# Feed-forward of a two-layer trunk: PSUM banks dealt out anew, five of seven weight operands and the activation sums copied through three of them

## The chip, the cores and the metric

The kernel runs on one core of a Trainium2 chip. TensorE (PE) multiplies, VectorE (DVE), ScalarE (ACT) and GpSimd (POOL) do the work on elements, and DMA queues, most of them issued by SyncE (SP), bring the weights from HBM. The metric is the device time of one execution in microseconds (us), as the median of repeated runs; lower is better. A profile is one such execution, recorded instruction by instruction.

## The reference, cut to what matters

The program is two layers of an attention mixer followed by a gated feed-forward with a causal convolution of width 3. 512 tokens, model width 1024, inner width 2816, all in fp32. The change touches the feed-forward only:

```python
def conv_ffn(h, w_gu, conv_w, conv_b, w_down):
    a, u = jnp.split(h @ w_gu, 2, axis=-1)
    a = causal_depthwise_conv(a, conv_w, conv_b)
    return (jax.nn.silu(a) * u) @ w_down

def reference(x, ...):
    for i in range(DEPTH):
        ...
        h = rms_norm(x, norm_ffn[i])
        x = x + conv_ffn(h, ffn_w_gu[i], ffn_conv_w[i], ffn_conv_b[i], ffn_w_down[i])
    return rms_norm(x, norm_final)
```

## The kernel before, in words

**Precision.** Every fp32 operand of a product is split into a high part, cast by ACT to the fp32r type, and a low part, the operand minus its high part, made by a subtraction on DVE or POOL. A product is three kinds of matmul: high with high, high with low, low with high. Tiles named h.. or wh are high parts, l.. or wl low parts.

**Feed-forward.** The inner width is cut into 22 column tiles f = 0 to 21 of 128. Of each, the gate half a and the up half u are wanted, 128 x 512 each. Tiles f = 0 to 2 take the plain way (gate_up, L205 for the matmuls): 24 matmuls of 512 columns for a and 24 for u. Tiles f = 3 to 21 (19 in a layer, 38 in all) take gate_up_7: tokens are cut into halves and the 2 x 2 product of (weight halves) x (token halves) is made with seven products instead of eight, numbered o = 0 to 6, each 12 matmuls of 256 columns (L619), 84 in all. Their left operands are the weights a1, a2, u1, u2 themselves (each 256 KB by its own DMA, L591) and sums of them: POOL makes s1 = u1 + u2, s2 = s1 - a1, s3 = a1 - u1, s4 = a2 - s2 (L596), of which s2 and s3 lie side by side in the tile "wraw". Each of the seven operands that is used (a1, s2, s3, a2, s1, s4, u2) is cast by ACT (L602) and subtracted by DVE (L608). The right operands are sums of the activations, built once in a layer while the plain tiles run (operands, L564 on): DVE scales, POOL makes four sums in a step, ACT casts (L579) and copies each pair of sums into a PSUM bank (L583), DVE subtracts (L585, tile "xs").

**After the products** of a tile f, in the order o = 0, 1, 3, 5, 2, 6, 4 into the four accumulators pa, pb, pc, pa, pb, pd, pc: ACT copies pa twice into the padded row tile "apad" (L629, L637), DVE adds the others (L623), ACT and DVE form the convolution in a PSUM tile py (L536, L537, L538), ACT applies Silu (L539), and POOL multiplies with u (L649, after which the result lies in g, xh or xl). After f = 21 the down projection follows, again with L205 matmuls into "mm" tiles; its operands are split on ACT (L670) and DVE (L671).

**PSUM.** All eight banks are in four rings: "mm" of 2, "s" of 2, "t" of 3 and "o" of 1. Every allocation with a tag takes the ring's next bank and waits until its former holder has been read for the last time. Which instruction stands where on an engine is decided by a scheduler when the program is built; SP issues the DMAs in an order that this also sets, and a DMA into a buffer waits in SP's queue for the last reader of that buffer's former content.

**What the change touches.** In `weights` (L588 on) the subtraction of a1 reads a copy of a1 that ACT has put in an "mm" bank, that of a2 a copy in "s", that of u2 a copy in "t" (L607). Those of s2, s3, s1 and s4 read both operands from SBUF. The accumulators pa, pb, pc, pd are in "mm", "s", "t", "o"; py is in "t", prs (the broadcast norm that L569 reads) in "t", and the copies of the activation sums go through the one bank of "o".

Of the kernel before, what the change touches and what calls it, by code (L numbers as in the profile page):

```python
# [11 lines left out]
F32 = mybir.dt.float32  # L12
# [5 lines left out]
P = 128  # L18
T = 512
# [12 lines left out]
B_MM, B_S, B_T, B_O = 2, 2, 3, 1  # L32
# [27 lines left out]
PLO = ((3, 6, 7), (3, 6))  # L60
BUFS = dict(a1=2, a2=2, u1=2, u2=2, s1=2, s4=2, ha1=2, la1=2, ha2=1, la2=1, hs1=1, ls1=1, hs4=1, ls4=1, hu2=1, lu2=1)
GL = [n for n in ("u1", "a1", "u2", "a2", "s1", "s4", "ha1", "la1", "ha2", "la2", "hs1", "ls1", "hs4", "ls4") for _ in range(BUFS[n])]
BANKS = dict(a1=("mm", B_MM), a2=("s", B_S), u2=("t", B_T))
CUES = (((), (0, 1), (2, 3, -1), (4, 5), (6, 7), (), ()), ((), (0, 1, 2), (3,), (4, 5, 6, -1), (7, 8), (), ()))
SCALE_SWA = "vvvv"
WARM_NSA, WARM_SWA = (54, 66)
# [73 lines left out]
def trunk(ctx: ExitStack, tc: tile.TileContext, x, w_nsa, w_gate, w_c1, w_c2, w_nsao, w_nsao3, w_swa, w_swao,  # L140
# [350 lines left out]
    with tc.tile_pool(name="tab", bufs=1) as pool:  # L491
        stats0 = ffn(tc, 0, locals())
        with tc.tile_pool(name="swa", bufs=1) as pool:
            cs = pool.tile([P, 2, T], F32, name="cs")
            vb = pool.tile([P, P], F32, name="vb")
            with tc.high_priority(offset=100):
                nc.sync.dma_start(cs, tabs)
                nc.sync.dma_start(vb, swa_vb)
            layer_now[0] = 1
            stats = Stats(pool, nc.gpsimd)  # L500
            swa(tc, locals())
            first = first_products(1, stats)
    ffn(tc, 1, locals())


def ffn(tc, layer, e):
    nc, wp, ps, V = e["nc"], e["wp"], e["ps"], e["V"]
# [4 lines left out]
    with tc.tile_pool(name=f"ffn{layer}", bufs=1) as pool:  # L512
# [3 lines left out]
        def conv(i):  # L516
            return conv_t[:, i:i + 1]
# [4 lines left out]
        def gated(f):  # L522
            k = f - NF + len(x_tags)
            n = f"g{f}" if k < 0 else f"{x_tags[k][0]}{x_tags[k][1]}"
            g[f] = (pool if k < 0 else e["cp"]).tile([P, T], F32, name=n, tag=n)
            return g[f]
# [5 lines left out]

        def activate(f, a):
            y = pool.tile([P, T], F32, name="y", tag="y", bufs=1)
            py = ps.tile([P, T], F32, name="t", tag="t", bufs=B_T)
            nc.scalar.activation(py, a[:, 2:], AF.Identity, scale=conv(f * 3 + 2), bias=conv(3 * NF + f))  # L536
            nc.vector.scalar_tensor_tensor(py, a[:, 1:T + 1], conv(f * 3 + 1), py, op0=ALU.mult, op1=ALU.add)  # L537
            nc.vector.scalar_tensor_tensor(py, a[:, 0:T], conv(f * 3), py, op0=ALU.mult, op1=ALU.add)  # L538
            nc.scalar.activation(y, py, AF.Silu)  # L539
            return y  # L540
# [6 lines left out]
        def gate_up(f):  # L547
            pa = plain(f, 0, "mm") if f else e["first"][0]
            a = apad[f % 2]
            nc.vector.tensor_tensor(a[:, 2:], pa, rstd, op=ALU.mult)  # L550
            y = activate(f, a)
            pu = plain(f, 1, "s") if f else e["first"][1]
            u = gated(f)
            nc.vector.tensor_tensor(u, pu, rstd, op=ALU.mult)
            nc.gpsimd.tensor_tensor(u, u, y, op=ALU.mult)
# [5 lines left out]
        def half(n, dt=F32R):  # L561
            return pool.tile([P, T], dt, name=n, tag=n, bufs=BUFS[n])

        def operands(i):  # L564
            n = [half(t, F32) for t in (("ha2", "hs4"), ("la2", "ls4"))[i % 2]]
            t = [half(t, F32).rearrange("p (o t) -> p o t", o=2) for t in (("hs1", "hu2"), ("ls1", "lu2"))[i % 2]]
            for h in range(2):
                k = i + h * NK // 2
                nc.vector.scalar_tensor_tensor(n[h], X[k], V(f"ffn{layer}", k), prs, op0=ALU.mult, op1=ALU.mult)  # L569
            x1l, x1r, x2l, x2r = (n[h][:, c] for h in range(2) for c in HALVES)  # L570
            t2, t1, t3, t4 = (t[j][:, h] for j in range(2) for h in range(2))
            eng = nc.gpsimd
            eng.tensor_tensor(t1, x1r, x1l, op=ALU.subtract)
            eng.tensor_tensor(t3, x2r, x1r, op=ALU.subtract)
            eng.tensor_tensor(t2, x2r, t1, op=ALU.subtract)
            eng.tensor_tensor(t4, x2l, t2, op=ALU.subtract)
            for o, src in ((slice(0, 1), x1l.unsqueeze(1)), (slice(5, 7), n[1].rearrange("p (o t) -> p o t", o=2)),
                           (slice(1, 3), t[0]), (slice(3, 5), t[1])):
                nc.scalar.copy(xs[:, o, i, 0], src)  # L579
                if o.stop - o.start == 2:  # L580

                    src2 = ps.tile([P, T], F32, name="o", tag="o", bufs=B_O).rearrange("p (o t) -> p o t", o=2)
                    nc.scalar.copy(src2, src)  # L583
                    src = src2
                nc.vector.tensor_tensor(xs[:, o, i, 1], src, f32(xs[:, o, i, 0]), op=ALU.subtract)  # L585

        def weights(f):
            a1, a2, u1, u2, s1, s4 = (half(n, F32) for n in ("a1", "a2", "u1", "u2", "s1", "s4"))  # L588
            for j, h, w in ((0, 0, a1), (1, 0, u1), (1, 1, u2), (0, 1, a2)):
                with tc.high_priority(offset=100):  # L590
                    nc.sync.dma_start(w, e["w_gu"][layer, j, f, :, h * T:(h + 1) * T])  # L591
            s23, l23, h23 = (wp.tile([P, 2, T], t, name=n, tag=n) for n, t in (("wraw", F32), ("wl", F32R), ("wh", F32R)))
            s2, s3 = (s23[:, h] for h in range(2))
            for out, x, y, op in ((s1, u1, u2, ALU.add), (s2, s1, a1, ALU.subtract), (s3, a1, u1, ALU.subtract),
                                  (s4, a2, s2, ALU.subtract)):
                nc.gpsimd.tensor_tensor(out, x, y, op=op)  # L596
            ws = {1: (h23[:, 0], l23[:, 0]), 3: (h23[:, 1], l23[:, 1])}
            for o, n, w in ((0, "a1", a1), (1, None, s2), (3, None, s3), (5, "a2", a2), (2, "s1", s1), (6, "s4", s4),
                            (4, "u2", u2)):
                if n:  # L600
                    ws[o] = half("h" + n), half("l" + n)
                nc.scalar.copy(ws[o][0], w)  # L602
                if n in BANKS:

                    tag, bufs = BANKS[n]
                    w = ps.tile([P, T], F32, name=tag, tag=tag, bufs=bufs)
                    nc.scalar.copy(w, {"a1": a1, "a2": a2, "u2": u2}[n])  # L607
                nc.vector.tensor_tensor(ws[o][1], w, f32(ws[o][0]), op=ALU.subtract)  # L608
            return ws

        def gate_up_7(f, cue):
            ws = weights(f)
            pa, pb, pc, pd = (ps.tile([P, T], F32, name=n, tag=n, bufs=b)[:, :H]
                              for n, b in (("mm", B_MM), ("s", B_S), ("t", B_T), ("o", B_O)))

            def product(pt, o, start=False):
                ops = [(0, x, i) for i in range(NK // 2) for x in range(2)] + [(1, 0, i) for i in range(NK // 2)]
                for n, (w, x, i) in enumerate(ops):
                    nc.tensor.matmul(pt, ws[o][w][:, i * P:(i + 1) * P], xs[:, o, i, x], start=start and n == 0,  # L619
                                     stop=n == len(ops) - 1, skip_group_check=True)  # L620

            def add(dst, pt, src):
                nc.vector.tensor_tensor(dst, pt, src, op=ALU.add)  # L623

            a, u = apad[f % 2], gated(f)
            al, ar = a[:, 2:2 + H], a[:, 2 + H:]
            ul, ur = (u[:, c] for c in HALVES)
            product(pa, 0, True)
            nc.scalar.copy(ar, pa)  # L629
            cue(0)  # L630
            product(pb, 1, True)
            add(ul, pb, ar)
            cue(1)
            product(pc, 3, True)
            cue(2)
            product(pa, 5)
            nc.scalar.copy(al, pa)  # L637
            cue(3)
            product(pb, 2)
            add(ar, pb, ar)  # L640
            add(ur, pc, ar)
            cue(4)
            product(pd, 6, True)
            add(ar, pd, ar)
            cue(5)
            product(pc, 4)
            add(ul, pc, ul)
            cue(6)
            nc.gpsimd.tensor_tensor(u, u, activate(f, a), op=ALU.mult)  # L649

        prs = ps.tile([P, T], F32, name="t", tag="t", bufs=B_T)
        nc.scalar.copy(prs, rstd)
        for f in range(PLAIN[layer]):
            gate_up(f)
# [25 lines left out]
        def cue(n):  # L680
            for f in CUES[layer][n]:
                if f < 0:
                    w_down.append(load_down(0, -1 - f))
                else:
                    split_g(f)
# [879 lines left out]
```

## Time and profile before

| | |
|---|---|
| median of three runs | 1295.8 us (1295.52 to 1297.48) |
| the profiled execution | 1297.73 us, span 1295.9 us |
| mean granted clock of TensorE | 0.982 |
| PE busy | 1228.0 us, 95% |
| DVE busy | 939.0 us, 72% |
| ACT busy | 760.1 us, 59% |
| POOL busy | 604.7 us, 47% |
| feed-forward of layer 0, tiles f = 3 on | about 405 to 626 us |
| feed-forward of layer 1, tiles f = 3 on | about 947 to 1167 us |

PE's share is a mean over stages. What the change can move is read in the two feed-forward stretches: how many matmuls PE gets done there in a stretch of time, what it waits for, and how the engines that make its operands follow one another.

### The profile page before, as it was taken

What the parts mean: (1) busy time and instruction counts of PE and PEld (TensorE: products, weight loads), DVE (VectorE), ACT (ScalarE), POOL (GpSimd) and SP (SyncE); (2) the same over time, 40 slices, a digit from 0 to 9 for tenths busy, and PEclk for the clock granted to TensorE, in tenths of its full rate; (3) what the DMA queues carried; (4) which work ended last, traced back from release to release, by engine and by line L of the source; (5) the groups of instructions that cost most, each with busy time, mean ns of one, the idle gap of its engine ahead of it and who ended that gap; (6) DMA issues with size and microseconds to landing.
All of it is one profiled execution on the core that took longest, in us unless ns stands there. A gap on an engine that the chain in (4) does not pass through costs nothing.

```text
span 1295.9 us, 20370 instructions
## 1 busy us (share of the span) xinstructions
PE 1228.0 (95%) x7246; PEld 1058.7 (82%) x7246; DVE 939.0 (72%) x1799; ACT 760.1 (59%) x1584; POOL 604.7 (47%) x451
## 2 busy tenths in 40 slices
PE   7999999989998999999999998999989999999997
PEld 5867986877876999999888886778779999998886
DVE  6376777978688897999633367897888999994223
ACT  4276667767558666767422225866677676683222
POOL 4494554523239676664100137322577766730002
PEclk9999999989998999999999998999989999999999
DMA  5856635041232332332233345322423332223333
GB/s 196 227 159 191 199 103 153 26 142 37 62 104 99 95 103 92 104 92 62 80 99 90 108 156 157 106 82 90 132 75 97 98 106 92 81 69 90 95 101 122
DMA packets 66485, 141.70 MB, mean 109 GB/s; under 512 B 8528, under 2 KB 16976, under 8 KB 66384
## 3 DMA queue, kind: packets, MB, share of 16 engines
q1 hardware_dynamic: 65008, 139.25, 35.5%
q8 instruction: 57, 0.93, 0.3%
q10 hardware_dynamic: 1376, 1.15, 0.3%
q14 instruction: 44, 0.36, 0.1%
HBM read 123.14 MB, written 17.24 MB: 108 GB/s over the span
## 4 chain that ended last, share of the span: by engine, by line
PE 53%; DVE 19%; DMA 7%; POOL 7%; ACT 7%; issue 5%; SPq 1%; POOLq 0%; DVEq 0%; ACTq 0%
PE mm L205 29%; PE t L619 4%; PE s L619 3%; DVE wl L608 3%; PE mm L619 3%; DMA u<-in_w_gu 2%; PE s L1165 2%; POOL s L596 2%; DVE ls L608 2%; PE o L619 2%; PE o L1007 2%; PE t L1189 2%; POOL wraw L596 1%; DMA d<-rh 1%; PE o L1307 1%
## 5 line engine op out<-in xcount | busy, mean ns | idle before, releaser
L182 ACT CAST wh<-wraw 128x1024 fp32r<-128x1024 f32 (+3 forms) x132 | 122.2, 926 | 224.5 <-PE mm L205 139.2
L183 DVE TENSOR_TENSOR wl<-wraw,wh 128x1024 fp32r<-128x1024 f32 (+3 forms) x80 | 98.0, 1225 | 118.7 <-PE mm L205 72.2
L183 POOL TENSOR_TENSOR wl<-wraw,wh 128x1024 fp32r<-128x1024 f32 (+3 forms) x52 | 98.7, 1902 | 136.5 <-PE mm L205 67.2
L205 PE MATMUL mm<-xs,wh 128*128 128x512 f32 (+1 forms) x374 | 141.5, 382 | 0.0
L238 POOL TENSOR_TENSOR rt<-rt 128x512 f32<-128x512 f32 x22 | 31.5, 1430 | 192.2 <-ACT rt L232 192.0
L608 DVE TENSOR_TENSOR wl<-wraw,wh 128x512 fp32r<-128x512 f32 x76 | 97.2, 1282 | 18.8 <-ACT wh L602 18.6
L205 PE MATMUL mm<-xh,wh 128*128 128x512 f32 x248 | 102.1, 413 | 6.9 <-ACT wh L182 5.1
L205 PE MATMUL mm<-xl,wh 128*128 128x512 f32 x248 | 99.9, 404 | 2.1 <-DVE xl L306 2.0
L619 PE MATMUL mm<-xs,ha 128*128 128x256 f32 x608 | 92.5, 289 | 9.4 <-ACT apad L629 4.8
L619 PEld LDWEIGHTS mm<-xs,ha 128*128 128x128 f32 x608 | 81.8, 195 | 12.3 <-ACT apad L629 6.2
L205 PE MATMUL mm<-xs,wl 128*128 128x512 f32 (+1 forms) x374 | 90.6, 382 | 0.0
L602 ACT CAST wh<-wraw 128x512 fp32r<-128x512 f32 x76 | 46.8, 620 | 69.4 <-POOL wraw L596 57.2
L1175 ACT ACTIVATE p<-p,sm 128x128 f32<-128x128 f32 (+3 forms) x128 | 71.7, 562 | 20.1 <-DVE sm L1172 19.5
L205 PEld LDWEIGHTS mm<-xs,wh 128*128 128x128 f32 x374 | 70.3, 188 | 14.7
L608 DVE TENSOR_TENSOR ls<-s,hs 128x512 fp32r<-128x512 f32 x76 | 80.2, 1060 | 0.0
L205 PEld LDWEIGHTS mm<-xs,wl 128*128 128x128 f32 x374 | 67.7, 188 | 15.1
L1172 DVE CUSTOM_DVE_ANT_0 p<-s,cst 128x128 f32<-128x128 f32 (+3 forms) x128 | 58.3, 480 | 18.1 <-PE t L1189 10.4
L205 PE MATMUL mm<-xh,wl 128*128 128x512 f32 x248 | 67.7, 403 | 0.0
L596 POOL TENSOR_TENSOR s<-u,u 128x512 f32<-128x512 f32 x38 | 53.2, 1401 | 27.1 <-DMA u<-in_w_gu 21.5
L649 POOL TENSOR_TENSOR xl<-xl,y 128x512 f32<-128x512 f32 x16 | 29.6, 1852 | 77.4 <-ACT y L539 69.9
L205 PEld LDWEIGHTS mm<-xh,wh 128*128 128x128 f32 x248 | 48.5, 196 | 18.8 <-ACT wh L182 5.3
L596 POOL TENSOR_TENSOR s<-a,wraw 128x512 f32<-128x512 f32 x38 | 62.8, 1653 | 0.2
(369 smaller groups left out, 3689.1 us busy)
## 6 DMA issues: line engine op xcount, KB each, us to landing
u<-in_w_gu SPq DMA_DIRECT2D x76, 256.0 KB, 2.9
a<-in_w_gu SPq DMA_DIRECT2D x76, 256.0 KB, 2.8
wraw<-in_w_dn SPq DMA_DIRECT2D x34, 512.0 KB, 3.5
wraw<-in_w_nsa SPq DMA_DIRECT2D x19, 512.0 KB, 4.9
q<-d SPq DMA_DIRECT2D x32, 256.0 KB, 5.1
wraw<-in_w_dn SPq DMA_DIRECT2D x17, 384.0 KB, 3.1
wraw<-in_w_gu SPq DMA_DIRECT2D x12, 512.0 KB, 3.5
d<-rh SPq DMA_DIRECT2D x21, 256.0 KB, 2.2
```

Source lines behind the costliest of these rows:

```text
L182: nc.scalar.copy(wh[:, c], raw[:, c])
L183: (eng or lo_eng[0]).tensor_tensor(wl[:, c], raw[:, c], f32(wh[:, c]), op=ALU.subtract)
L205: nc.tensor.matmul(pt, ws[k][w], rs[k][r], start=first and i == 0, stop=last and i == len(ops) - 1, **kw)
L238: self.eng.tensor_tensor(self.acc, self.acc, sq, op=ALU.add)
L596: nc.gpsimd.tensor_tensor(out, x, y, op=op)
L602: nc.scalar.copy(ws[o][0], w)
L608: nc.vector.tensor_tensor(ws[o][1], w, f32(ws[o][0]), op=ALU.subtract)
L619: nc.tensor.matmul(pt, ws[o][w][:, i * P:(i + 1) * P], xs[:, o, i, x], start=start and n == 0, stop=n == len(ops) - 1, skip_group_check=True)
L649: nc.gpsimd.tensor_tensor(u, u, activate(f, a), op=ALU.mult)
L1007: nc.tensor.matmul(acc[0][:, j * P:], v2[:, 2 * j + br], pp[:, 4 * j:4 * j + NT - j, :], start=br == 0 and j == 0 and pp is pts[0][0], sto ...
L1172: nc.vector.tensor_tensor_reduce(pt[:, c], pss[:, c], mask[:, T - (c.stop - c.start):], -1.0, 3e38, ALU.add, ALU.min, st[:, u:u + 1])
L1175: nc.scalar.activation(pt[:, c], pt[:, c], AF.Exp, scale=-1.0, bias=st[:, u:u + 1], accum_out=st[:, 2 + u:3 + u])
```

## The change

All that the change does is to move tiles between the four rings and to add copies. Of the seven weight operands five now have a copy in a bank of "t" ahead of their subtraction: a1, a2 and u2, which had one in other rings, and s2 and s3, which were read from SBUF. The copy reads the operand itself, from whatever tile it lies in. The copies of the activation sums also go through the three banks of "t". The accumulators leave "t": pa is in "o", pb and pd in "mm", pc in "s"; so is py, and prs is in "o".

```diff
-BANKS = dict(a1=("mm", B_MM), a2=("s", B_S), u2=("t", B_T))
+BANKS = (0, 1, 3, 5, 4)
...
         def activate(f, a):
...
-            py = ps.tile([P, T], F32, name="t", tag="t", bufs=B_T)
+            py = ps.tile([P, T], F32, name="s", tag="s", bufs=B_S)
...
-                    src2 = ps.tile([P, T], F32, name="o", tag="o", bufs=B_O).rearrange("p (o t) -> p o t", o=2)
+                    src2 = ps.tile([P, T], F32, name="t", tag="t", bufs=B_T).rearrange("p (o t) -> p o t", o=2)
...
                 nc.scalar.copy(ws[o][0], w)
-                if n in BANKS:
-
-                    tag, bufs = BANKS[n]
-                    w = ps.tile([P, T], F32, name=tag, tag=tag, bufs=bufs)
-                    nc.scalar.copy(w, {"a1": a1, "a2": a2, "u2": u2}[n])
+                if o in BANKS:
+
+                    pw = ps.tile([P, T], F32, name="t", tag="t", bufs=B_T)
+                    nc.scalar.copy(pw, w)
+                    w = pw
                 nc.vector.tensor_tensor(ws[o][1], w, f32(ws[o][0]), op=ALU.subtract)
...
-                              for n, b in (("mm", B_MM), ("s", B_S), ("t", B_T), ("o", B_O)))
+                              for n, b in (("o", B_O), ("mm", B_MM), ("s", B_S), ("mm", B_MM)))
...
-        prs = ps.tile([P, T], F32, name="t", tag="t", bufs=B_T)
+        prs = ps.tile([P, T], F32, name="o", tag="o", bufs=B_O)
```

ACT gets 76 instructions more (two copies for each of 38 tiles f); the counts of the other engines stay. The scheduler also places instructions anew inside the feed-forward, as three places show. A name's number tells one buffer from the next; the copy line is L607 before and L606 after.

ACT's row around the weights of tile f = 13 in layer 0 (wh_5759 before, wh_5799 after, are the high parts of its s2 and s3), before:

```order
L602 CAST wh_5759<-wraw_5757 128x512
L602 CAST ha1_5914<-a1_5897 128x512
L602 CAST wh_5759<-wraw_5757 128x512
L629 COPY apad0_3990<-mm_5644 128x256
L536 ACTIVATE t_5591<-apad1_3991,conv_t_3988 128x512
L607 COPY t_5641<-u2_5600 128x512
L602 CAST hu2_5638<-u2_5600 128x512
```

and of the change:

```order
L602 CAST wh_5799<-wraw_5797 128x512
L606 COPY t_5811<-wraw_5797 128x512
L606 COPY t_5815<-wraw_5797 128x512
L602 CAST ha1_5958<-a1_5941 128x512
L629 COPY apad0_3990<-o_5684 128x256
L606 COPY t_5821<-a2_5788 128x512
L536 ACTIVATE s_5627<-apad1_3991,conv_t_3988 128x512
L606 COPY t_5835<-u2_5790 128x512
L602 CAST hu2_5678<-u2_5636 128x512
```

Two copies of the wraw halves stand between the second cast of wh and the instructions that lead to the next hu2, and every copy takes a bank of the one ring "t".

PE's row at the end of layer 0's plain tiles (mm_4037, mm_4181: gate halves of f = 1 and 2; s_4075, s_4219: up halves of f = 1 and 2; mm_4294 before, o_4298 after: pa of f = 3), before:

```order
L205 MATMUL mm_4037<-xh7_80,wl_4033 128x512
L205 MATMUL s_4075<-xh0_73,wh_4070 128x512
...
L205 MATMUL s_4075<-xh7_80,wl_4071 128x512
L205 MATMUL mm_4181<-xh0_73,wh_4176 128x512
...
L205 MATMUL mm_4181<-xh7_80,wl_4177 128x512
L205 MATMUL s_4219<-xh0_73,wh_4214 128x512
...
L619 MATMUL mm_4294<-xs_3994,ha1_4264 128x256 x8
```

and of the change:

```order
L205 MATMUL mm_4037<-xh7_80,wl_4033 128x512
L205 MATMUL mm_4181<-xh0_73,wh_4176 128x512
...
L205 MATMUL mm_4181<-xl7_88,wh_4176 128x512
L205 MATMUL s_4075<-xh0_73,wh_4070 128x512
...
L205 MATMUL mm_4181<-xh7_80,wl_4177 128x512
L619 MATMUL mm_4299<-xs_3994,wh_4259 128x256 x4
L619 MATMUL o_4298<-xs_3994,ha1_4264 128x256 x8
L619 MATMUL mm_4299<-xs_3994,wh_4259 128x256
L205 MATMUL s_4219<-xh0_73,wh_4214 128x512
```

The gate half of f = 2 now starts ahead of the up half of f = 1, and thirteen matmuls of f = 3 ahead of the up half of f = 2.

DVE's row while the activation sums are built in layer 0 (xs is the tile of right operands; wl, la1, la2, ls4, ls1 are low parts of weights of f = 3 and 4), before:

```order
L608 TENSOR_TENSOR wl_4258<-wraw_4257,wh_4259 128x512
L585 TENSOR_TENSOR xs_3994<-o_4120,xs_3994 128x2x256
L537 SCALAR_TENSOR_TENSOR t_4208<-apad0_3990,conv_t_3988,t_4208 128x512
L608 TENSOR_TENSOR la1_4415<-mm_4417,ha1_4414 128x512
L538 SCALAR_TENSOR_TENSOR t_4208<-apad0_3990,conv_t_3988,t_4208 128x512
L585 TENSOR_TENSOR xs_3994<-o_4124,xs_3994 128x2x256
L554 TENSOR_TENSOR g2_4244<-s_4219,rstd_89 128x512
L608 TENSOR_TENSOR wl_4408<-wraw_4407,wh_4409 128x512 x2
L585 TENSOR_TENSOR xs_3994<-o_4140,xs_3994 128x2x256
```

and of the change:

```order
L585 TENSOR_TENSOR xs_3994<-t_4140,xs_3994 128x2x256
L585 TENSOR_TENSOR xs_3994<-t_4144,xs_3994 128x2x256
L537 SCALAR_TENSOR_TENSOR s_4208<-apad0_3990,conv_t_3988,s_4208 128x512
L538 SCALAR_TENSOR_TENSOR s_4208<-apad0_3990,conv_t_3988,s_4208 128x512
L585 TENSOR_TENSOR xs_3994<-t_4148,xs_3994 128x2x256
L585 TENSOR_TENSOR xs_3994<-t_4164,xs_3994 128x2x256
L554 TENSOR_TENSOR g2_4244<-s_4219,rstd_89 128x512
L608 TENSOR_TENSOR ls4_4289<-s4_4252,hs4_4288 128x512
L585 TENSOR_TENSOR xs_3994<-t_4168,xs_3994 128x2x256
L608 TENSOR_TENSOR ls1_4285<-s1_4251,hs1_4284 128x512
L585 TENSOR_TENSOR xs_3994<-t_4172,xs_3994 128x2x256
L608 TENSOR_TENSOR la1_4265<-t_4267,ha1_4264 128x512
```

The sums' subtractions stand closer together and the weights' subtractions that read a bank of "t" stand behind them.

## Rows read from the trace of the kernel before

**Rows 1.** The page: busy time, share of the span and instructions of the engines.

```profile
PE 1228.0 (95%) x7246; PEld 1058.7 (82%) x7246; DVE 939.0 (72%) x1799; ACT 760.1 (59%) x1584; POOL 604.7 (47%) x451
```

**Rows 2.** Stretches of both feed-forwards: length, busy time (instructions) by engine, clock, DMA.

```profile
405.00:437.00 32.00, 26.40 (x185) 24.87 (x185) 24.43 (x40) 23.51 (x46) 21.55 (x19) 0.84 0.23 75
437.00:470.00 33.00, 33.00 (x277) 32.92 (x276) 28.76 (x46) 23.96 (x47) 25.49 (x18) 1.00 0.37 112
470.00:590.00 120.00, 112.44 (x912) 109.75 (x912) 106.60 (x154) 79.34 (x153) 82.98 (x56) 1.00 0.30 93
947.00:980.00 33.00, 27.02 (x191) 25.38 (x191) 26.53 (x43) 24.48 (x47) 22.25 (x19) 0.90 0.22 73
1010.00:1130.00 120.00, 113.27 (x919) 110.20 (x918) 110.62 (x153) 79.86 (x153) 84.54 (x57) 1.00 0.32 97
```

**Rows 3.** Waits of PE from 470 to 612 us: total, times, longest.

```profile
PE t L619 <- DVE xh L623: 3.1, 3, 1.4
PE mm L619 <- DVE la L608: 1.2, 1, 1.2
...
PE mm L619 <- ACT apad L629: 1.0, 2, 0.8
```

**Rows 4.** DVE's subtractions at L608, 470 to 612 us: duration min/median/max, first and last start.

```profile
L608 DVE TENSOR_TENSOR ls<-s,hs x26: 677/1127/1800, 474.9 to 608.6; 128x512 fp32r<-128x512 f32 x26
L608 DVE TENSOR_TENSOR wl<-wraw,wh x25: 691/1443/1789, 468.6 to 600.2; 128x512 fp32r<-128x512 f32 x25
L608 DVE TENSOR_TENSOR la<-mm,ha x12: 675/686/692, 473.9 to 596.2; 128x512 fp32r<-128x512 f32 x12
```

**Rows 5.** Waits of ACT from 470 to 612 us: total, times, longest.

```profile
ACT wh L602 <- POOL wraw L596: 22.0, 11, 3.9
ACT y L539 <- DVE t L538: 12.3, 10, 2.3
ACT t L536 <- DVE apad L623: 9.6, 8, 2.0
```

**Rows 6.** The chain that ended last, 565 to 582 us: start, us, what.

```profile
570.25 0.53 ACT hu L602
...
570.79 3.03 DMA u<-in_w_gu
...
573.89 1.71 POOL s L596
...
575.68 1.64 POOL wraw L596
...
577.33 0.63 ACT wh L602
```

**Rows 7.** POOL's multiplication among its groups, 440 to 610 us: line and operation, count, busy us, mean ns.

```profile
L649 POOL TENSOR_TENSOR xh<-xh,y 128x512 f32<-128x512 f32 x8 | 10.4, 1298 | 19.6 <-ACT y L539 19.6
```

**Rows 8.** Timeline of ACT behind that chain: start, us, what.

```profile
577.33 0.62 ACT L602 CAST wh<-wraw 128x512 fp32r<-128x512 f32 x1 [2.85 <-POOL wraw L596]
...
579.36 0.58 ACT L607 COPY t<-u 128x512 f32<-128x512 f32 x1
579.87 0.62 ACT L602 CAST hu<-u 128x512 fp32r<-128x512 f32 x1
```

**Rows 9.** Waits of DVE from 405 to 437 us: total, times, longest.

```profile
DVE xs L585 <- ACT o L583: 3.8, 4, 1.6
```

**Rows 10.** Timeline of ACT over layer 0's plain tiles: start, us, what.

```profile
389.83 1.05 ACT L182 CAST wh<-wraw 128x1024 fp32r<-128x1024 f32 x1
```

**Rows 11.** Timeline of PE there and at the end of f = 21: start, us, what.

```profile
388.74 0.39 PE L205 MATMUL s<-xh,wh 128*128 128x512 f32 x1
...
612.46 0.39 PE L205 MATMUL mm<-xs,wh 128*128 128x512 f32 x1
```

**Rows 12.** Timeline of DVE at the last activation sum and at the end of f = 21.

```profile
420.75 0.68 DVE L585 TENSOR_TENSOR xs<-o,xs 128x512 fp32r<-128x512 f32 x1
...
618.96 0.41 DVE L623 TENSOR_TENSOR apad<-s,apad 128x256 f32<-128x256 f32 x1
```

## The prediction

> **What bounds the kernel now.** I read the page first, then the two feed-forwards cut into stretches, then the waits of PE there, and last the engines that PE waits for. On the page the reader sees a PE that is busy 95% of the span and a DVE at 72% [rows 1]; that is a mean, and the change touches two stretches only. In the stretches one looks at the number of matmuls. From 437 to 470 us PE does 277 in 33 us, 0.119 us each, with the clock at 1.00 [rows 2]. A tile of 84 matmuls so takes at least 84 x 0.119 = 10.0 us. From 470 to 590 us it does 912 in 120 us, that is 11.05 us a tile, and in layer 1 from 1010 to 1130 us 919, 10.97 us a tile [rows 2]: about 1.0 us of each tile is lost, and 470 to 612 us holds 142 / 11.05 = 12.9 such tiles, in layer 1 I take as many. The two starts lose more in less time: from 405 to 437 us 185 matmuls come instead of 269, which is 84 x 0.119 = 10.0 us, from 947 to 980 us 191 instead of 277, 10.3 us; the granted clock falls to 0.84 and 0.90 there [rows 2].
>
> Who makes PE wait in the steady part? The waits name DVE for the larger ones (its additions at L623 that free accumulators, its low parts at L608) and ACT's copies of pa [rows 3]. DVE is busy 106.6 of 120 us there, 110.6 in layer 1 [rows 2], which is 9.8 to 10.1 us a tile: without a gap it would be just as long as PE. It is so long because of one sort of instruction. A subtraction whose operand lies in PSUM takes 0.675 to 0.692 us, always; those with both operands in SBUF (wl for s2 and s3, ls for s1 and s4) have the same minimum, 0.691 and 0.677, but a median of 1.443 and 1.127 and reach 1.8 us [rows 4]. They run while POOL makes its sums, and POOL's own sums take 1.64 to 1.71 us in the same stretch [rows 6] against 1.298 for its multiplication, of the same shape [rows 7]. So DVE and POOL hold each other up.
>
> **What each part costs.** *Two copies in place of two SBUF reads.* For DVE each tile loses 2 x (1.443 - 0.686) = 1.5 us, from about 10.0 to 8.5. The bounds for one subtraction are 0 (the minima are alike) and 1.789 - 0.675 = 1.1 us; I take the medians, since 25 instructions make them. The minima of 0.691 and 0.675 say that a source in PSUM is no slower [rows 4]. The Trainium skill, in VectorE: DVE Perf Modes, section Why PSUM operands drop a tier, speaks against the change: an operand in PSUM holds an fp32 operation to the lowest rate. Were an SBUF subtraction alone to run at twice the rate, the change would pay only for the contention beyond it; the rows do not show such a faster one. The skill's SBUF — State Buffer, section SBUF: two separate sides, has a DVE operation with two SBUF inputs and a GpSimd operation that reads SBUF shut one another out for a whole instruction. By it a blocked subtraction gives back up to a whole POOL instruction, 2.6 us a tile by 1.298, where the medians give 1.5; the loop below would set the tile by either. Two subtractions of the four, those of s1 and s4, stay as they are.
>
> For ACT each tile gets two copies more. A copy takes 0.58 us and the next instruction starts 0.51 us after it [rows 8], so 2 x 0.51 = 1.0 us a tile (bounds 1.0 and 1.2). ACT is busy 79.3 of 120 us [rows 2], 7.3 us a tile, and waits another 22.0 + 12.3 + 9.6 = 43.9 us in 12.9 tiles, 3.4 a tile: for POOL's s2 and s3, for the convolution on DVE and for DVE's additions [rows 5]. All of these lie behind the instructions that become shorter, so the 1.0 us have a cover of 3.4. If that cover does not give way, they are added to the tile in full.
>
> *The loop that decides.* The chain of waits shows what is late next. ACT casts u2 (start 570.25); that frees its buffer, u comes in by DMA (3.03), POOL adds s1 (1.71) and s2 (1.64), ACT casts wh at 577.33 [rows 6], and on ACT's row the next cast of u2 starts at 579.87 [rows 8]: one round is 9.62 us when nothing else stands in it. The change puts its two copies of the wraw halves between wh and that cast (+1.0), and POOL's two sums may shrink from 3.35 towards 2.6 us; I take half of that, -0.35, as two SBUF subtractions remain. 9.62 + 1.0 - 0.35 = 10.3 us. PE's own 10.0 is close below, DVE's 8.5 well below. Since the scheduler does not place every round alike I add 0.15: 10.45 us a tile. From 11.0 that is 0.55 x 12.9 x 2 = **14 us gained**. The bounds are 10.0 (26 us) and no gain.
>
> *The ring of three.* Five copies of a tile go round three banks, so a copy waits for the subtraction three copies earlier; behind it on ACT stand L629 and L637, on which pa, now in the single bank of "o", depends: PE waits for them once they are later than the 24 to 32 matmuls between two uses of pa allow, 24 x 0.119 = 2.9 us. Today copies of pa cost PE 1.0 us from 470 to 612 us, with two banks [rows 3]. I allow for one such wait more per layer, **2 us lost**; below, 0, above, one in every tile (that is a rival).
>
> *Start.* From 405 to 437 us DVE waits 3.8 us for ACT's copies in the one bank "o" [rows 9], and it makes its last sum at 420.75 [rows 12]. With three banks those waits can go, and the last sum comes up to 3.8 us earlier, near 417. Against it stands the new order on PE. The gate half of f = 2 needs weights whose cast runs from 389.83 for 1.05 us [rows 10], and PE would come to it at 388.74, where it now does the up half of f = 1 [rows 11]: 390.88 - 388.74 = 2.1 us of new wait. Also, the weights of f = 3 now stand behind the sums in DVE's row. Of the 10 us lost in each start I count 1 us net as recovered, **2 us gained** in both (bounds: 2 lost and 4 gained in each).
>
> *Tail.* The down projection begins at 612.46 among the last products of f = 21 [rows 11]; it uses "mm", which pb and pd now hold, so it waits for DVE's addition from pb, which comes at 618.96 today and takes 0.41 us [rows 12]. That product work moves rather than grows; what is lost is the addition with its handing over, 0.5 to 1.5 us a layer: **2 us lost** in both. The other moves (py to "s", prs to "o") only follow from these and cost nothing by themselves: py's work on ACT and DVE is the same and lies beside matmuls; if pc and py delay each other in "s", it shows as a longer round, which the 0.15 covers.
>
> **Sum.** 14 - 2 + 2 - 2 = 12 us. The profiled execution of 1297.73 us would become 1285.7; the median of 1295.8 is 1.9 us below that execution, and 1295.8 - 12 = 1283.8, so I say **1284**.
>
> **Rivals.** *A, the forecast:* rounds of 10.3 to 10.6 us, 1279 to 1290; chance 0.53. *B, PE becomes the bound:* rounds of 10.0, all 26 us of the steady part come, with the other terms 1272 or a little less. For it speaks that 437 to 470 us already runs so; against it, that the loop has 1.0 us more on ACT. Chance 0.17. *C, nothing gained:* the round through u's DMA, POOL and ACT keeps its length, because POOL's sums stay as long as they are and the copies take what DVE gives; the tile stays at 11.0, and start, ring and tail nearly cancel: 1294 to 1298. For it speaks that the longest idle of ACT is behind POOL, not behind DVE [rows 5]; chance 0.12. *D, ACT becomes the bound:* the wait of a copy for a bank of "t" holds up the copies of pa and the convolution behind it. ACT's busy time would be 7.3 + 1.0 = 8.3 us; this case decides from the point where its waits of 3.4 us a tile shrink by less than the 1.0 us of new copies. If they shrink by half of that, a tile is 0.5 us longer: 0.5 x 25.8 = 13 us slower, 1309; if not at all, 26 us, 1322. For it speaks the single bank of pa. Chance 0.18.
>
> **Numbers.** Faster by over 0.2% (2.6 us, about what a measurement of this kernel tells from no change): A and B, 0.70. Within it: C, 0.12. Slower: D, 0.18. The range goes from B's end to beyond C, where D's mild cases begin: 1270 to 1300. The likeliest case alone is 1279 to 1290.
>
> **What would show it.** DVE's subtractions for wl at 0.68 us everywhere; those for ls still above 1; POOL's sums nearer 1.3; some 960 matmuls in 120 us of the steady part instead of 912 to 919 (10.45 us a tile); ACT waiting less for wraw, with DVE's subtractions as a new releaser before its copies; a new wait of PE of about 2 us in the plain tiles; the last sum near 417. The forecast is wrong if PE's waits for L629 and L637 grow to over 0.5 us a tile, if the two copies are followed by idle PE, or if the starts, with their lower clock, get longer.

## The result and the profile after

| | before | after |
|---|---|---|
| median of six runs each | 1295.74 us (1290.75 to 1297.48) | 1282.69 us (1275.94 to 1285.90) |
| ratio | | 0.990, 95% interval 0.9873 to 0.9927 |
| the profiled execution, its span | 1297.73 us, 1295.9 us | 1280.34 us, 1278.6 us |

The forecast was 1284 us, faster. Single runs of the changed kernel spread over 10 us, so what follows rests on medians, ratios with their intervals, and on what the traces show of the steady part.

The page of the changed kernel, busy time by engine, answers to [rows 1]:

```profile
PE 1220.3 (95%) x7246; PEld 1055.7 (83%) x7246; DVE 906.8 (71%) x1799; ACT 797.4 (62%) x1660; POOL 580.0 (45%) x451
```

ACT has 37 us more, DVE 32 us less, and POOL, whose instructions did not change, 25 us less. Stretches of the changed kernel, columns as in [rows 2]; the last one is of layer 1:

```profile
405.00:437.00 32.00, 29.77 (x207) 27.93 (x206) 27.75 (x44) 27.69 (x55) 21.47 (x19) 0.95 0.31 99
437.00:470.00 33.00, 33.00 (x278) 33.00 (x277) 27.31 (x48) 27.86 (x54) 21.71 (x16) 1.00 0.30 97
470.00:590.00 120.00, 118.41 (x986) 117.88 (x985) 101.57 (x164) 97.27 (x187) 82.73 (x59) 1.00 0.32 100
1003.00:1123.00 120.00, 117.73 (x984) 117.12 (x983) 102.32 (x164) 96.78 (x188) 82.03 (x59) 1.00 0.31 100
```

In the same 120 us PE does 986 matmuls instead of 912, 10.22 us a tile of 84 instead of 11.05, and in layer 1 984 instead of 919. DVE's busy time for a tile is 101.57 / (986 / 84) = 8.65 us instead of 9.82, ACT's 8.29 instead of 7.31.

DVE's subtractions from 470 to 612 us, as in [rows 4]:

```profile
L608 DVE TENSOR_TENSOR ls<-s,hs x26: 681/1368/1782, 473.5 to 597.5; 128x512 fp32r<-128x512 f32 x26
...
L608 DVE TENSOR_TENSOR wl<-t,wh x24: 673/680/693, 477.5 to 589.8; 128x512 fp32r<-128x512 f32 x24
```

The subtractions that now read PSUM take 0.68 us without exception; the two that still read SBUF are as slow as before or slower. The waits of PE and of ACT in the same stretch, as in [rows 3, 5]:

```profile
PE s L619 <- DVE xl L623: 0.8, 1, 0.8
PE mm L205 <- DVE apad L623: 0.8, 1, 0.8
PE s L619 <- DVE xh L623: 0.8, 1, 0.8
```

```profile
ACT ha L602 <- PE o L619: 7.1, 7, 1.5
ACT hs L602 <- PE mm L619: 5.8, 10, 0.8
ACT wh L602 <- POOL wraw L596: 4.0, 6, 1.2
```

```profile
DVE apad L623 <- PE mm L619: 10.9, 10, 1.5
```

ACT waited 22.0 us for POOL's s2 and s3 and now 4.0; its largest wait, and DVE's, is now for PE. The engines that PE waited for now wait for PE. The chain that ended last says the same of 470 to 590 us: PE's matmuls are 94.9% of it, and the subtractions of s2 and s3 (wl), 12.2% of it in the kernel before, are not in it.

```profile
by line: PE mm L619 39.5%; PE s L619 28.7%; PE o L619 26.7%; DVE ls L608 3.0%; issue 1.6%; DVE xh L623 0.3%; DVE xl L623 0.3%; DVE apad L623 0.0%
```

How DVE and POOL hold each other up can be read in the trace of the kernel before, by laying the starts and ends of the two engines side by side:

```profile
522.59 1.75 POOL L596 TENSOR_TENSOR s<-a,wraw 128x512 f32<-128x512 f32 x1
523.10 1.79 DVE L608 TENSOR_TENSOR wl<-wraw,wh 128x512 fp32r<-128x512 f32 x1
...
528.31 1.74 POOL L596 TENSOR_TENSOR s<-u,u 128x512 f32<-128x512 f32 x1
528.82 1.78 DVE L608 TENSOR_TENSOR wl<-wraw,wh 128x512 fp32r<-128x512 f32 x1
```

POOL's first sum here ends at 524.34 and the subtraction at 524.89, the second at 530.05 and 530.60: 0.55 us later both times. From 437 to 612 us, 51 subtractions with both operands in SBUF start while an instruction of POOL has more than 0.13 us to go, and all 51 end 0.55 to 0.56 us after that instruction does: the subtraction waits for POOL's whole instruction. In return POOL's instructions that start while such a subtraction runs have a median of 1.72 us (44 of them), those that meet none 1.30 us (12 of them, from 437 to 600 us).

Where the 17 us between the two profiled executions lie is read by counting L619 matmuls in the timelines. From the first matmul of f = 1 (383.3 us before, 381.9 after) to the last L619 matmul, layer 0 takes 242.0 and 234.3 us, layer 1 241.8 and 235.9 us: 13.6 us together, about the difference of the medians. The remaining 3.7 us lie before and between these stretches; the two profiled executions lie 2.0 us above and 2.4 us below their medians, so this is no more than the spread of single runs. Inside the layers:

| from, to | layer 0 before, after | layer 1 before, after |
|---|---|---|
| f = 1 to the end of the first 84 | 41.7, 42.6 | 42.0, 42.5 |
| 85th to 420th (four tiles) | 40.3, 40.2 | 40.1, 41.1 |
| 421st to 1260th (ten tiles) | 109.1, 102.8 | 108.7, 103.7 |
| 1261st to the last (four tiles, with the first of the down projection) | 50.9, 48.7 | 51.0, 48.6 |

The gain lies behind the 420th matmul; the start became a little longer.

### The profile page after: what moved, and what is told of

The parts are those of the page before. It is cut to its first block, busy times and chain, and to the rows that moved or that the text cites. A ratio compares the mean times of both kernels' runs of the same rounds, so it can differ in the third digit from the quotient of the medians.

```text
span 1278.6 us, 20545 instructions
## 1 busy us (share of the span) xinstructions
PE 1220.3 (95%) x7246; PEld 1055.7 (83%) x7246; DVE 906.8 (71%) x1799; ACT 797.4 (62%) x1660; POOL 580.0 (45%) x451
## 4 chain that ended last, share of the span: by engine, by line
PE 67%; DVE 13%; POOL 6%; DMA 5%; issue 5%; ACT 2%; SPq 1%; POOLq 0%; DVEq 0%; ACTq 0%
PE mm L205 29%; PE mm L619 11%; PE s L619 8%; PE o L619 7%; PE s L1165 2%; PE o L1007 1%; PE t L1189 1%; DVE ls L608 1%; PE o L1307 1%; DVE xl L306 1%; DMA q<-d 1%; DMA d<-rh 1%; DVE p L1184 1%; PE t L1409 1%; DMA d<-rl 1%
## 5 line engine op out<-in xcount | busy, mean ns | idle before, releaser
L205 PE MATMUL mm<-xh,wh 128*128 128x512 f32 x248 | 104.4, 423 | 12.3 <-ACT wh L182 11.3
L608 DVE TENSOR_TENSOR ls<-s,hs 128x512 fp32r<-128x512 f32 x76 | 89.9, 1190 | 3.1 <-ACT hs L602 1.9
L619 PE MATMUL o<-xs,ha 128*128 128x256 f32 x608 | 87.2, 287 | 2.2 <-DVE ls L569 1.7
L619 PE MATMUL mm<-xs,hs 128*128 128x256 f32 x608 | 87.8, 283 | 0.3 <-DVE apad L623 0.3
L619 PEld LDWEIGHTS o<-xs,ha 128*128 128x128 f32 x608 | 79.9, 195 | 2.8 <-DVE ls L569 2.1
L619 PEld LDWEIGHTS mm<-xs,hs 128*128 128x128 f32 x608 | 79.2, 191 | 0.6 <-DVE apad L623 0.5
L596 POOL TENSOR_TENSOR wraw<-a,u 128x512 f32<-128x512 f32 x38 | 59.4, 1563 | 6.5 <-DMA a<-in_w_gu 3.4
```

The source lines that it names most:

```text
L205: nc.tensor.matmul(pt, ws[k][w], rs[k][r], start=first and i == 0, stop=last and i == len(ops) - 1, **kw)
```

## The experiments

Each kernel was timed beside the kernel before on the same chip, and its ratio is to those runs. Runs of different chips are compared by these ratios. The table has each result, and from its profile the steady stretch from 470 to 590 us of layer 0, divided by its number of tiles (matmuls / 84).

| run | median us | ratio to before, interval | us per tile | DVE busy per tile | ACT busy per tile |
|---|---|---|---|---|---|
| before | 1296 | 1 | 11.05 | 9.82 | 7.31 |
| the change | 1282.69 | 0.990 (0.9873 to 0.9927) | 10.22 | 8.65 | 8.29 |
| e1, three copies | 1311.26 | 1.013 (1.010 to 1.016) | 10.89 | 9.88 | 7.30 |
| e2, five, old banks | 1275.52 | 0.985 (0.982 to 0.988) | 10.03 | 8.33 | 8.35 |
| e3, seven copies | 1273.52 | 0.984 (0.981 to 0.987) | 10.03 | 7.69 | 9.30 |
| e4, plain tiles' order | 1283.34 | 0.992 (0.989 to 0.995) | 10.23 | 8.63 | 8.45 |
| e5, seven, old banks | 1279.23 | 0.987 (0.984 to 0.990) | 10.03 | 7.57 | 9.19 |
| e6, unread copies, old banks | 1279.35 | 0.988 (0.984 to 0.991) | 10.23 | 9.56 | 8.19 |
| e7, new accumulators, old copies | 1340.45 | 1.035 (1.032 to 1.038) | 11.83 | 9.64 | 7.50 |
| e8, e1 with pa in "mm" | 1308.56 | 1.010 (1.007 to 1.014) | 10.73 | 9.76 | 7.18 |
| e9, unread copies, new banks | 1311.90 | 1.012 (1.008 to 1.016) | 11.05 | 10.53 | 8.36 |
| e10, s4 first | 1291.32 | 0.996 (0.994 to 0.999) | 10.62 | 9.74 | 7.37 |
| e11, e3 with s4 first | 1272.86 | 0.982 (0.978 to 0.987) | 10.03 | 7.68 | 9.29 |
| e12, e1 with sums in "o" | 1311.70 | 1.013 (1.009 to 1.017) | 11.02 | 9.97 | 7.37 |

**e1: the new banks without the two new copies.**

```diff
-BANKS = (0, 1, 3, 5, 4)
+BANKS = (0, 5, 4)
```

> The changed kernel with its new banks, but only a1, a2 and u2 copied into the ring of three; s2 and s3 are subtracted from SBUF again. Theory 1 (DVE relieved: the two subtractions that leave SBUF no longer meet POOL's sums): the steady tile goes back from 10.3 to about 10.9 us, 0.6 x 26 tiles = 15 us, so about 1297 us, and wl is back at a median of 1.4 us. Rival 2 (the new dealing of banks frees accumulators earlier, the copies only follow): stays at 1283 or falls a little, since ACT has 76 copies fewer.

1311 us: theory 1 had the direction, but the kernel is not back at the kernel before, it is 17 us slower than it. So the change is two things with opposite signs: banks that cost and copies that give back more. The steady stretch of e1:

```profile
470.00:590.00 120.00, 114.44 (x926) 111.41 (x925) 108.94 (x156) 80.43 (x155) 80.29 (x54) 1.00 0.32 97
```

That is 10.89 us a tile, no longer than before. The cost lies mostly elsewhere: from f = 1 to the last L619 matmul e1 takes 18.8 us more in both layers together, of which 11.9 lie ahead of the 421st matmul, 2.1 in the ten tiles behind it and 4.8 in the last four. In the kernel before, the four tiles behind the first run at PE's pace, 10.1 us each, and the slow ones come later; in e1 they take 11.1 on average. Why is asked in e7, e8 and e12.

**e2: the copies without the new banks.**

```diff
-BANKS = dict(a1=("mm", B_MM), a2=("s", B_S), u2=("t", B_T))
+BANKS = dict(a1=("mm", B_MM), a2=("s", B_S), u2=("t", B_T), s2=("s", B_S), s3=("t", B_T))
...
+                    src, (tag, bufs) = w, BANKS[m]
...
```

> The kernel before with its old banks, and copies of s2 (into ring s) and s3 (into ring t) added; nothing else moves. Theory 1: wl falls to 0.68 us and the steady tile to about 10.3 us, start and tail stay as before: about 1281 us. Rival 2: no gain without the new banks, 1296 us, or slower by up to 13 us, since the copies compete with accumulators for their banks.

1275.5 us, below theory 1's 1281, and better than the change (0.985 against 0.990, with intervals that overlap a little): the two copies in the banks of before are enough, and the new banks are not needed. Rival 2 falls. The steady stretch:

```profile
470.00:590.00 120.00, 120.00 (x1005) 120.00 (x1005) 99.63 (x169) 99.93 (x192) 81.55 (x60) 1.00 0.32 98
```

PE waits for nothing; 1005 matmuls in 120 us are its own pace, 10.03 us a tile.

**e3: all seven copied, new banks.**

```diff
-BANKS = (0, 1, 3, 5, 4)
+BANKS = (0, 1, 2, 3, 4, 5, 6)
```

> The changed kernel with all seven operands copied into the ring of three (s1 and s4 too). Theory 1: DVE loses another 2 x (1.37 - 0.68) = 1.4 us a tile, but PE is only 0.3 us a tile above its 10.0, so at most 7 us come: 1276 to 1283 us. Rival 3 (ACT and the ring of three are the next bound): ACT gets 1.0 us more a tile, 9.1 us busy of 10.3, copies wait for banks and PE for copies of pa: 1286 to 1300 us.

1273.5 us, 2.5 us below theory 1's range; rival 3 falls, ACT carries 9.3 us of a tile of 10.0 and PE does not wait. This run shows the contention itself, by its absence. DVE's subtractions from 470 to 612 us, and POOL's sums from 440 to 610 us:

```profile
L608 DVE TENSOR_TENSOR ls<-t,hs x26: 680/681/692, 470.9 to 590.2; 128x512 fp32r<-128x512 f32 x26
L608 DVE TENSOR_TENSOR la<-t,ha x25: 679/681/693, 470.0 to 586.6; 128x512 fp32r<-128x512 f32 x25
L608 DVE TENSOR_TENSOR wl<-t,wh x24: 679/684/691, 476.0 to 585.4; 128x512 fp32r<-128x512 f32 x24
```

```profile
L596 POOL TENSOR_TENSOR wraw<-s,a 128x512 f32<-128x512 f32 x15 | 19.5, 1300 | 0.2
L596 POOL TENSOR_TENSOR s<-a,wraw 128x512 f32<-128x512 f32 x15 | 19.5, 1299 | 0.1
L596 POOL TENSOR_TENSOR wraw<-a,u 128x512 f32<-128x512 f32 x14 | 18.2, 1297 | 0.0
```

With no subtraction that reads SBUF twice, every subtraction takes 0.68 us and every sum of POOL 1.30 us. Nobody changed POOL's instructions. The Trainium skill, SBUF — State Buffer, section SBUF: two separate sides, has a DVE operation with two SBUF inputs and a GpSimd operation that reads SBUF take one port pair in turn; the traces agree: of the kernel before, by the 51 subtractions above, and here, by the median of ls (1.37 us in the change, 0.68 here) and the mean of POOL's s3 (1.62 us in the change, 1.30 here). In e5, with its old banks, the sums' means are 1.30 us as well.

**e4: the plain tiles' order restored.** py of f = 0 to 2 is in the ring "t", of the others in "s".

```diff
+            tag, bufs = ("t", B_T) if f < PLAIN[layer] else ("s", B_S)
-            py = ps.tile([P, T], F32, name="s", tag="s", bufs=B_S)
+            py = ps.tile([P, T], F32, name=tag, tag=tag, bufs=bufs)
```

> The changed kernel with py of the three plain tiles back in the ring of three, which restores PE's old order of the plain tiles. Theory 4 (the start lost because of that order: PE waited 3.1 us for a cast at 390.7): 2 to 3 us come back in each layer, 1277 to 1279 us. Rival 5 (the start lost because the weights of f = 3 come behind the activation sums): the wait only moves behind the plain tiles, 1282 to 1284 us.

1283.34 us, ratio 0.992 (0.989 to 0.995), as the change. The wait of 3.1 us for the cast is gone, and in the first products stand other waits of PE (375 to 437 us):

```profile
PE s L620 <- ACT xs L580: 3.2, 1, 3.2
PE o L620 <- DVE la L609: 1.9, 1, 1.9
```

Rival 5 holds: the wait moved behind the plain tiles, where PE meets the activation sums and the low parts of f = 3.

**e5: all seven copied, old banks** (s1 in "mm", s4 in "s", beside e2's).

```diff
-... s2=("s", B_S), s3=("t", B_T))
+... s2=("s", B_S), s3=("t", B_T), s1=("mm", B_MM), s4=("s", B_S))
```

> The kernel before with its old banks and all seven operands copied: s2 and s4 in ring s, s3 in ring t, s1 in ring mm. Theory 1 (time comes from subtractions that leave SBUF, and PE is the floor): PE already has no wait in the steady part with five copies in old banks, so the time stays near that of e2, 1272 to 1278 us; all subtractions take 0.68 us and POOL's sums 1.30 us. Rival 3 (copies crowd out accumulators from their rings): PE waits for mm and s again, 1285 us or more.

1279.2 us, slightly above the range, with an interval that overlaps those of e2 and e3: beyond five copies nothing is left to gain, since PE is at its pace.

**e6: e2's copies, read by nobody.** The copy is made, the subtraction reads SBUF.

```diff
                     nc.scalar.copy(w, src)
+                    if not n:
+                        w = keep
```

> The kernel of e2, but the copies of s2 and s3 are read by nobody: the subtractions read SBUF as before. It has ACT's 76 copies and their banks, and none of the relief. Theory 1: no gain over the kernel before; at best equal (1294), up to 26 us slower if ACT's 1.0 us a tile is not hidden. Rival 6 (the gain of e2 comes from another order that the copies bring about): 1276 to 1285 us.

1279.4 us, inside rival 6's range. In the old banks the two copies bring 16 us even if nobody reads them, so theory 1 as it stood falls there; what reading them adds (e2 against e6, 0.985 against 0.988) is within the intervals. DVE's row shows what happened (470 to 612 us):

```profile
L612 DVE TENSOR_TENSOR ls<-s,hs x26: 677/1252/1781, 473.0 to 596.9; 128x512 fp32r<-128x512 f32 x26
L612 DVE TENSOR_TENSOR wl<-wraw,wh x24: 678/1168/1779, 474.6 to 588.8; 128x512 fp32r<-128x512 f32 x24
```

The subtractions still meet POOL, but wl less (1.168 us instead of 1.443): DVE's busy time is 9.56 us a tile instead of 9.82, which is below PE's 10.03. The copies brought about another order on every engine: in POOL's row the s3 of the next tile now stands behind s4, where POOL waits 10.0 us in all for the copy that reads "wraw", and ACT's wait for the convolution (y at L539, 12.3 us before) is 0.2.

```profile
POOL wraw L596 <- ACT t L609: 10.0, 10, 2.7
```

**e7: the new accumulators with the copies in their old rings.**

```diff
-BANKS = (0, 1, 3, 5, 4)
+BANKS = dict(a1=("mm", B_MM), a2=("s", B_S), u2=("t", B_T))
...
```

The edit is against the change: accumulators, py, prs and the sums' copies stay in their new places. The copy of u2 is in "t" in every kernel; only those of a1 and a2 go back to other rings. 

> The change's new places for accumulators, py, prs and the activation sums, with the three copies of before in their old rings (a1 in mm, a2 in s, u2 in t). e1 was 18 us slower than before with all banks new. Theory 7 (the new accumulators cost it: pb and pd share mm, pc and py share s, pa has one bank): as slow as e1 or slower, since the copies crowd them more, 1305 to 1330 us. Rival 8 (the single ring of three for all copies costs it): back to 1292 to 1297 us.

1340.45 us, ratio 1.035 (1.032 to 1.038). Theory 7's direction, and 10 us above its range; rival 8 falls. PE's waits from 470 to 612 us are now for the accumulators in "s", where pc, py and the copy of a2 share two banks, and in "o":

```profile
PE s L619 <- DVE xl L623: 6.3, 3, 2.1
PE s L619 <- DVE xh L623: 6.3, 3, 2.1
PE o L619 <- ACT apad L637: 3.3, 6, 0.7
```

So with these places of the accumulators the copies of a1 and a2 do better in the ring of three than in "mm" and "s".

**e8: e1 with pa and pb in "mm", pd alone in "o".**

```diff
-                              for n, b in (("o", B_O), ("mm", B_MM), ("s", B_S), ("mm", B_MM)))
+                              for n, b in (("mm", B_MM), ("mm", B_MM), ("s", B_S), ("o", B_O)))
```

> The kernel of e1 (new banks, three copies), but pa and pb share mm and pd is alone in o. In e1 PE waited 4.7 us for additions before an mm bank from 470 to 612 us. Theory 9 (the pair pb and pd in mm is what costs e1 its 18 us, because pb of the next tile waits for the addition from pd): most of it comes back, 1293 to 1300 us. Rival 10 (pc and py in s, or the ring of the copies): stays at 1306 to 1313 us.

1308.56 us, ratio 1.010 (1.007 to 1.014), inside rival 10's range: theory 9 falls, the pair of pb and pd in "mm" is not most of the cost.

**e9: the change with two copies that nobody reads.** The subtractions of s2 and s3 read SBUF.

```diff
-                    w = pw
+                    w = w if n is None else pw
```

> The changed kernel with all its copies and banks, but the subtractions of s2 and s3 read SBUF, as before; the two copies are read by nobody. Beside the changed kernel it takes away the relief of DVE alone; in POOL's row s3 of the next tile stays ahead of s4 and the multiplication ahead of s1. Theory 1 (relief): the steady tile goes back to 10.9 us or longer, 1297 to 1311 us, as e1. Rival 6 (the copies bring about a better order, as they did in e6): 1280 to 1286 us.

1311.9 us, 0.9 us above theory 1's range, so rival 6 falls here, and the same as e1 (the ratios are 1.012 and 1.013): the two copies on ACT alone cost nothing that can be measured and bring nothing, and reading them is worth 2.2%, about 28 us, in the new banks. The order changes with it: in the steady part of the change, in both layers, POOL's multiplication stands behind s1 or behind s3 in two of three rounds of POOL's row, here ahead of s1 in all. Its steady stretch and wl:

```profile
470.00:590.00 120.00, 113.10 (x912) 109.93 (x911) 114.35 (x153) 90.81 (x174) 81.56 (x55) 1.00 0.30 96
```

```profile
L608 DVE TENSOR_TENSOR wl<-wraw,wh x26: 674/1496/1784, 470.7 to 607.9; 128x512 fp32r<-128x512 f32 x26
```

DVE is busy 114.35 of 120 us, 10.53 us a tile: more than PE's 10.03. Here DVE itself is the bound, as one round of the chain that ended last shows (start, us, what):

```profile
503.80 1.78 DVE wl L608
505.58 0.33 DVE xh L623
505.92 1.36 DVE ls L608
507.27 0.34 DVE apad L623
507.61 1.37 DVE wl L608
...
514.83 1.78 DVE wl L608
```

The round takes 514.83 - 503.80 = 11.03 us, as long as the tile, and both subtractions wl lie in it with 3.15 us. At 0.68 us each, as when they read the copies, they would take 1.36 and the round, by this estimate, 9.2 us, which is less than PE's 10.03. So in these banks the two long subtractions set the tile, and the copies pay because they are read. That the other order adds something is not excluded; no run has the order of the change without the reading. What e6's copies did for the order, these do not: s3 of the next tile stays ahead of s4 in POOL's row.

**e10: the kernel before with s4 held ahead of the next s3 on POOL.**

```diff
-                nc.gpsimd.tensor_tensor(out, x, y, op=op)
+                with tc.issue_after(s4_of[-1].ins) if out is s3 and s4_of else nullcontext():
+                    ins = nc.gpsimd.tensor_tensor(out, x, y, op=op)
+            s4_of.append(ins)
...
```

> The kernel before, with one thing held: POOL makes s3 of the next tile behind s4 of this one, the order that the kernels of e2 and e6 have and the kernel before has not. No copy is added. Theory 11 (a loop of three tiles in POOL's row: the multiplication of tile f waits for y and stands just ahead of s1 of tile f + 3; s4 leads to the product before y, so one POOL sum of 1.3 to 1.75 us leaves the loop): 33 us for three tiles become 31.5, half a us a tile, 13 us: 1279 to 1285 us. Theory 1 alone (only relief of DVE counts): 1292 to 1297 us.

1291.3 us, 0.4% (0.1 to 0.6) faster, between the two ranges. POOL's row now has e6's order, s1, s2, s4, s3. That order counts, but for under a third of what e6 gained; the size of theory 11 was off, and where the rest of e6's gain comes from is not shown. The scheduler moved instructions on the other engines here too. Layer 0's tile is 10.62 us, layer 1's 10.90, with DVE at 9.74 and 10.12.

**e11: e3 with that order.** Edit as in e10, on e3. 

> The kernel of e3 (new banks, seven copies) with the same order of s4 ahead of the next s3. PE has no wait in its steady part, so theory 1 and theory 11 both expect the steady part unchanged and at most the start to move: 1270 to 1276 us. If it is slower by more, the earlier s4 has a price of its own (s3 later, o = 3 is the third product): 1277 us and more.

1272.86 us, ratio 0.982 (0.978 to 0.987), as expected: where PE is the bound, the order is worth nothing. It is level with e3.

**e12: e1 with the activation sums in "o" and prs in "t".**

```diff
-                    src2 = ps.tile([P, T], F32, name="t", tag="t", bufs=B_T).rearrange("p (o t) -> p o t", o=2)
+                    src2 = ps.tile([P, T], F32, name="o", tag="o", bufs=B_O).rearrange("p (o t) -> p o t", o=2)
-        prs = ps.tile([P, T], F32, name="o", tag="o", bufs=B_O)
+        prs = ps.tile([P, T], F32, name="t", tag="t", bufs=B_T)
```

> The kernel of e1 (new banks, three copies), but the activation sums go through the one bank of o again and prs through t, as before; this puts the low parts of a1 and a2 of f = 3 and 4 ahead of the last sums in DVE's row, as in the kernel before. In e1 tiles 4 to 7 behind the start took 44.3 and 44.4 us against 40.3 and 40.1 before, the tiles from 8 on no longer than before. Theory 12 (the sums that rotate through the ring of three push the first weights back, so PE starts without the lead that DVE and POOL had built up): tiles 4 to 7 take 40 to 41 us again and 8 to 12 us come back, 1299 to 1303 us. Rival 7 (the accumulators and py in fewer banks cost it): stays at 1307 to 1313 us, and tiles 4 to 7 at 44 us.

1311.7 us, as rival 7 said: theory 12 falls. Tiles 4 to 7 take 43.2 and 43.1 us, 1 us less than in e1, and the first 84 matmuls take 2 to 3 us more. Neither the sums' ring (e12) nor the pair in "mm" (e8) is what makes the new banks cost 17 us without the relief. e8 took pa out of its single bank as well, where it shared two with pb. The common ring of the three copies and pc with py in "s" are left, and combinations; which of them it is stays open.

## Why the prediction was right, point by point

- **The bound.** Right: PE's pace of 10.0 us and a DVE of 9.8 to 10.1 us with no gap to spare. The runs sharpen it. With DVE at 8.8 us a tile or less (the change, e2 to e5, e11) a tile takes 10.0 to 10.2 us; at 9.6 (e6) 10.2; at 9.6 to 10.5 (before, e1, e8, e9, e10, e12) 10.6 to 11.1. DVE's share is not all of it: e7, with DVE at 9.64, takes 11.83, and PE waits there for accumulators.
- **Two copies in place of two SBUF reads: DVE minus 1.5 us, to 8.5.** wl measured 0.68 as forecast, no slower than the 0.69 of the shortest one from SBUF, so no price of a source in PSUM shows. DVE 8.65: minus 1.2. The medians had priced wl too high: by the means it fell from 1.37 to 0.68 us, and ls rose from 1.13 to 1.25. ACT 8.29, as forecast (7.3 + 1.0), and its waits gave the cover.
- **The loop that decides, 10.45 us a tile, 14 us.** The ten steady tiles came out at 10.28 and 10.37 us by the count of matmuls, the windows at 10.22 and 10.24. The matmuls from the 85th on gained 8.6 and 6.4 us, 15 us together: the term was right in size. Its mechanism was only half right, and the size partly luck. ACT's wait for wraw fell from 22.0 to 4.0 us as said, but e2 has the same two copies on ACT and runs at PE's pace, so the copies between wh and the cast of u2 do not set the round. Nor does the change run in rounds of 10.3: counted tile by tile, fourteen of the twenty steady tiles take 10.0 to 10.2 us and the other six 10.5 to 11.3. The mean comes near 10.45 because a few tiles lose up to a microsecond, which none of e2's, in the old banks, does.
- **The ring of three, 2 us lost.** No such loss: no wait of PE for L629 or L637 is left in the steady part, and e3 with seven copies in three banks shows none. Too pessimistic by 2 us.
- **The start, 2 us gained.** Wrong in sign: 0.9 and 0.5 us lost from f = 1 to the end of the first 84. The wait for the cast was 3.1 us (2.1 forecast) and 2.4 in layer 1. That the starts get longer was one of the prediction's own signs of being wrong; the loss was only too small to move the total. The last sum came at 415.07 us, 5.7 earlier, and was worth little: e4 took the wait away, and PE then waited for a cast of the sums and for a1's low part instead.
- **The tail, 2 us lost.** PE waited 0.8 us for the addition in each layer, 1.6 together; as forecast.
- **What the sum did not have.** The new banks have a price that depends on the rest. Without the relief they cost 17 us (e1, e9), with it about 6 (the change against e2, by ratios 0.990 and 0.985). I gave all bank moves together 2 us lost. The sum came out because two errors met: a loop that was to hold the tile at 10.45 and does not, and a price of the banks in the steady tiles that was put at next to nothing. Against e2's pace of 10.03 the first is worth 0.4 us a tile and the second, what the ten steady tiles take more, 0.3.

Rival B (PE becomes the bound) came true in full in e2 and e3. In the change it did in fourteen of the twenty steady tiles, without the 26 us. Rivals C and D did not come true.

## What to carry to other kernels

Where two engines read the same memory, look at the spread of one instruction's duration, not at its mean: a minimum of 0.69 and a median of 1.44 us for the same shape say that half the time is somebody else's, and that moving one operand elsewhere can pay for an extra copy. When a change bundles a relief with a rearrangement, undo each alone: here the rearrangement was a cost of 17 us under a gain of about 28, and the two copies alone in the old places made the better kernel. A scheduler reorders whatever it is given, so an edit meant to isolate a cost (copies that nobody reads) can bring a gain of its own through another order; compare the rows before naming a cause.

## What was not expected of the hardware

A subtraction on DVE with both operands in SBUF that meets an instruction of POOL ends 0.55 us behind it, 51 times of 51: the price of such a meeting depends on where in POOL's instruction it begins, from next to nothing to 1.1 us. Two copies that nobody reads made the old kernel 16 us faster (e6); DVE and POOL met less there (wl 1.168 instead of 1.443 us), in another order on every engine, of which POOL's part alone gave under a third (e10). And ACT could be busy 111.2 of 120 us in e3 without one wait of PE from 470 to 590 us, while beside a DVE that was busy 106.6 of 120 us PE lost a tenth of its matmuls in the kernel before.
